# Output projection, second norm and down product with channels on the partitions, in a hybrid attention and SwiGLU block

## The chip, the core and the metric

One core of a Trainium2 chip runs the whole block in one launch. Its engines work side by side: TensorE (PE: matmuls, and PEld for its weight loads), VectorE (DVE), ScalarE (ACT), GpSimd (POOL) and SyncE (SP, which here only issues DMAs). The metric is the device time of one execution in microseconds, the median of several runs. The time before is 1010.89 us (three runs, 1010.83 to 1011.81).

## The reference, cut to what matters

```python
def rms_norm(x, g):
    y = xf * lax.rsqrt(jnp.mean(xf * xf, axis=-1, keepdims=True) + EPS)
    return y * g

def reference(x, ...):            # x: 1 x 1024 tokens x 1024 channels, float32
    h = rms_norm(x, norm1_g)
    q, k, v, u = split(h @ w_in)  # 512 wide each
    a = neighbourhood_attention(rms_norm(q), rms_norm(k), v, rpb)
    p = multiscale_pool(u, w_pool, pool_scale)
    x = x + concat([a, p]) @ w_out
    h2 = rms_norm(x, norm2_g)
    x = x + (silu(h2 @ w_gate) * (h2 @ w_up)) @ w_down   # 1024 -> 2816 -> 1024
    return x
```

The sum of squares of the second norm runs over the channels of one token.

## The kernel before

All products run in a reduced float32 format with each operand split into a high and a low half (`split`: ScalarE casts the high half, VectorE subtracts to get the low one); one product is three matmuls, high by high, high by low, low by high (`mm3`, `product`, `down`). The gate, up and down products are done as 2x2 block products with seven instead of eight multiplications: operands "11", "12", "21", "22" are blocks, and "s1" to "s4" (of the weights) and "t1" to "t4" (of the activations) are sums and differences of blocks. `sum_w` and the "s4" line of `cook_w` form the weight sums on POOL; `cook_w` splits them. The activations' blocks: the first half of the tokens (512) and the second half, by the first 512 channels and the last.

Around the change the program runs in these stages:

- Attention, interleaved with the projection (`g_dense`). `w_out(t, nh, cs, n)` adds up the output projection of token tile t (128 tokens) and channel half nh in a PSUM bank `pw`, and one VectorE add (L814) adds it to the residual in `x2[t]`, a tile of 128 tokens by 1024 channels that a DMA has filled with x.
- The second norm (`norm2(tt)`, two token tiles at a time). ScalarE issues the DMA that parks `x2[t]` in `x2d`, squares it with a running sum per token (L954), and Ln and Exp of two numbers per partition give the reciprocal root (L96, L97). VectorE scales the tile by the token's factor and by the channels' weights `g2b` (L962).
- Turns. The gate and up products need channels on the partitions, so `turn_op` turns each 128x128 block on TensorE into a PSUM bank `ht` (`tr`, L90), and `split` reads it from there into the operand `ACTO[o]`, called b11, bt2 and so on (`b`, `bt` in the profile). Each of seven operands takes 16 turns: 112. For the second half of the tokens the differences are formed before the turn: a0, t2 on VectorE (L975, L976), two more on POOL (L977, L978).
- The gate and up products. Index i runs over 22 blocks (gate and up in turn). For the first four (EARLY) the program does `first` and `second` (PSUM bank `x`, operands "11" and "21", which need the first half's norm alone) for all four, and then the rest of each (`rest`: banks `y`, `z`, `w`, operands t2, t3, t1, t4, 22, all of which need the second half). ScalarE takes Silu of the gate (L1056), VectorE or POOL multiplies (L1060). Results are parked in DRAM (`park`, `gsd`).
- The down product (`down`, `PLAN`): again seven products in three groups; its results are added to `x2` loaded back from `x2d`, and `ship` sends them out.

The order on each engine is set when the program is built, by a scheduler that plays the program through, except where the program pins it (attention, down product). PSUM has eight banks: pools `mmp` (3), `stp` (4), `pop` (1). SBUF tiles come from 45 slots that are used in turn, so a DMA into a slot waits for the last reader of what was there.

Of the kernel before, what the change touches and what calls it, by code (L numbers as in the profile page):

```python
# [9 lines left out]
F32 = mybir.dt.float32  # L10
# [39 lines left out]
def hybrid_block(ctx, tc, xT, xt, w1, wu, rpbx, wpool, wout, wgu, wd, g2, sm, out):  # L50
# [21 lines left out]
    sm_sb = cp.tile([P, 14], F32, name="sm_sb")  # L72
    g1_sb, psc_sb, gqk = sm_sb[:, 0:8], sm_sb[:, 8:12], sm_sb[:, 12:14]
# [724 lines left out]
    def w_out(t, nh, cs, n):  # L798
        ps = bank(stp if n else mmp, f"pw_{t}_{nh}_{n}")
        ns = slice(nh * 512, nh * 512 + 512)  # L800
        ts_ = slice(t % 4 * P, t % 4 * P + P)
        hf = t // 4
# [11 lines left out]
        nc.vector.tensor_tensor(out=x2[t][:, ns], in0=ps, in1=x2[t][:, ns], op=ALU.add)  # L814
# [5 lines left out]
    def g_dense():  # L820
# [5 lines left out]
        x2.extend(slot(F32, f"x2_{t}") for t in range(4))  # L826
        for t in range(4):
            nc.sync.dma_start(out=x2[t], in_=xt[t])
# [18 lines left out]
        for t in range(4):  # L847
# [4 lines left out]
            x2.append(slot(F32, f"x2_{4 + t}"))  # L852
            nc.sync.dma_start(out=x2[4 + t], in_=xt[4 + t])
# [52 lines left out]
    for t in range(4):  # L906
        for nh in range(2):
            for _ in w_out(t, nh, (2, 3), 1):
                pass
# [5 lines left out]
    sm2 = ctx.enter_context(tc.tile_pool(name="sm2", bufs=3))  # L915
    rg = ctx.enter_context(tc.tile_pool(name="rg", bufs=RING))
    x2d = [dp.tile([P, DM], F32, name=f"x2d_{t}") for t in range(NT)]
    gsd = [dp.tile([7, P, 512], F32, name=f"gsd_{f}") for f in range(NPF)]
    g2b = slot(F32, "g2b")
    nc.sync.dma_start(out=g2b, in_=g2.to_broadcast([P, DM]))  # L920
    junk = slot(F32, "junk")
    banks2 = (mmp, mmp, pop)
    nbk = 0
    ACTO = {}
    h2 = {}
# [6 lines left out]
    def turn_op(o, tt, srcs):  # L932
        nonlocal nbk
        ts_ = slice(tt % 2 * 256, tt % 2 * 256 + 256)
        for q in range(2):
            pt = bank(banks2[nbk % 3], f"ht_{o}_{tt}_{q}")
            nbk += 1
            for s in range(2):
                for i in range(2):
                    k = 2 * q + s  # L940
                    tr(
                        pt[:, s * 256 + i * P : s * 256 + i * P + P], srcs[i][:, k * P : k * P + P], ident
                    )
            hi, lo = ACTO[o][q]
            split(hi[:, :, ts_], lo[:, :, ts_], pt.rearrange("p (s n) -> p s n", s=2))

    def norm2(tt):
        v = sm2.tile([P, 16], F32, name=f"v2_{tt}", tag="v2")[:, :2]
        y = sm2.tile([P, 16], F32, name=f"y2_{tt}", tag="y2")[:, :2]
        for i in range(2):  # L950
            t = 2 * tt + i
            ss = sm2.tile([P, 16], F32, name=f"s2_{t}", tag="s2")[:, :1]
            nc.scalar.dma_start(out=x2d[t], in_=x2[t])
            nc.scalar.activation(junk, x2[t], AF.Square, accum_out=ss)  # L954
            nc.vector.tensor_scalar(
                out=v[:, i : i + 1], in0=ss, scalar1=1.0 / DM, scalar2=EPS, op0=ALU.mult, op1=ALU.add
            )
        rsqrt(sm2, y, v, 2, f"h{tt}")
        for i in range(2):
            t = 2 * tt + i  # L960
            h2[t] = x2[t]
            nc.vector.scalar_tensor_tensor(  # L962
                out=h2[t], in0=x2[t], scalar=y[:, i : i + 1], in1=g2b, op0=ALU.mult, op1=ALU.mult
            )
        if tt < 2:
            for o, j in (("11", 0), ("21", 1)):
                turn_op(o, tt, [h2[2 * tt + i][:, 512 * j : 512 * j + 512] for i in range(2)])
            return
        t2 = slot(F32, f"t2_{tt}", [P, 2, 512])
        lows, highs = [], []  # L970
        for i in range(2):
            t = 2 * tt + i
            a, b_ = h2.pop(t - 4), h2.pop(t)
            a0, a1, b0, b1 = a[:, :512], a[:, 512:], b_[:, :512], b_[:, 512:]
            nc.vector.tensor_tensor(out=a0, in0=b0, in1=a0, op=ALU.subtract)  # L975
            nc.vector.tensor_tensor(out=t2[:, i], in0=b1, in1=a0, op=ALU.subtract)  # L976
            nc.gpsimd.tensor_tensor(out=b0, in0=b1, in1=b0, op=ALU.subtract)  # L977
            nc.gpsimd.tensor_tensor(out=a1, in0=a1, in1=t2[:, i], op=ALU.subtract)  # L978
            lows.append((a0, a1))
            highs.append((b0, b1))  # L980
        src = {
            "t2": [t2[:, 0], t2[:, 1]],
            "t3": [h[0] for h in highs],
            "t1": [h[0] for h in lows],
            "22": [h[1] for h in highs],
            "t4": [h[1] for h in lows],
        }
        for o in src:
            turn_op(o, tt - 2, src[o])
# [81 lines left out]
    def rest(i, y, z, w, after, mid=None):  # L1071
        a, b_ = res[i]
        u2, u3 = a[:, 1], b_[:, 1]
# [3 lines left out]
        add(u2, ps, u2)  # L1077
        pz = bank(z, f"z_{i}")
# [38 lines left out]
    norm2(0)  # L1117
    norm2(1)
    for i in range(2):
        fetch_w(i)  # L1120
        cook_w(i, "11")
        cook_w(i, "12")
        sum_w(i)
    for nh in range(2):
        for t in range(6 - 2 * nh, 8):
            for _ in w_out(t, nh, eight, 2):
                pass
    for o in ("t2", "t3", "t1", "22", "t4"):
        act_op(o)
    norm2(2)  # L1130
    norm2(3)
    xs = [bank(stp, f"x_{i}") for i in range(EARLY)]
    for i in range(EARLY):
        if i == 2:
            for j in range(2, EARLY):
                fetch_w(j)
                cook_w(j, "11")
                cook_w(j, "12")
                sum_w(j)
# [4 lines left out]
    ring = (stp, stp, mmp, stp, stp)  # L1144
    nrk = 0
    LATE = ("s2", "s3", "s1", "22", "s4")
    for o in LATE:
        cook_w(0, o)
    for i in range(EARLY):
# [3 lines left out]
        three = []  # L1153
        for _ in range(3):
            three.append(ring[nrk % 5])
            nrk += 1
        nxt = i + 1

        def after(o):
            cook_w(nxt, o)  # L1160
            if nxt == EARLY and o == "s2":
                cook_w(nxt, "11")
            if nxt == EARLY and o == "s1":
                cook_w(nxt, "12")

        rest(i, *three, after)
# [3 lines left out]
    for i in range(EARLY, len(MF)):  # L1170
# [12 lines left out]
        rest(i, *yzw, after, mid=lambda: second(i, ps))  # L1183
# [6 lines left out]
    def quad(c, i, l):  # L1190
        return x2[c + 4 * i][:, 512 * l : 512 * l + 512]
# [101 lines left out]
    def ship(c, i, l, n0=0, n1=512):  # L1293
        t = c + 4 * i
        ns = slice(512 * l + n0, 512 * l + n1)
        nc.sync.dma_start(out=out[t][:, ns], in_=x2[t][:, ns])
# [11 lines left out]
    for t in range(NT):  # L1308
        x2[t] = slot(F32, f"x2r_{t}")
# [105 lines left out]
```

## Time and profile before

| | |
|---|---|
| median of 3 runs | 1010.89 us |
| profiled execution: time, span | 1011.3 us, 1009.5 us |
| PE busy | 997.8 us (99%), 4905 matmuls |
| DVE, ACT, POOL busy | 660.4, 415.8, 387.9 us |
| granted TensorE clock | 1.00 |

The span is the time from the first to the last instruction; about 2 us of the execution's time lie around it. Rows of a timeline give start, duration, engine, line, operation, what is written and read (out<-in), the shape, and in square brackets how long the engine stood idle before it and what ended that. The groups by line give count, busy time, mean ns, and idle time before. A matmul's duration includes its way through the array, so the distance of two starts is what it costs.

### The profile page before, as it was taken

The page shows a single profiled execution, that of the slowest core. Times are in us where ns is not written, and L with a number is a line of the kernel's source. Part 1 is how long each engine was busy: PE and PEld are TensorE (multiplying, and loading weights), DVE is VectorE, ACT ScalarE, POOL GpSimd, SP SyncE. Part 2 cuts the span into 40 slices and gives each one's busy share as a digit, 9 for nine tenths or more (in the row PEclk, how much of TensorE's full clock was granted, in tenths as well). Part 3 has the DMA queues.
Part 4 walks back from the last instruction along what each step waited for, and adds up shares of the span by engine and source line. Part 5 has one row for each costly group of instructions (what it writes and reads, how often), then busy time and mean ns, then how long its engine had stood idle before and what let it go on. Part 6 is the DMA issues. An engine that isn't in the chain of part 4 may idle for free.

```text
span 1009.5 us, 13495 instructions
## 1 busy us (share of the span) xinstructions
PE 997.8 (99%) x4905; PEld 851.1 (84%) x4905; DVE 660.4 (65%) x1087; ACT 415.8 (41%) x817; POOL 387.9 (38%) x427
## 2 busy tenths in 40 slices
PE   9999999999999998999999999999999999999998
PEld 9988989998888887888888888888888888888887
DVE  5677777657853769668555555555462599888872
ACT  6633666656642346333233233233242255442500
POOL 0001534332520436367846846846733400000170
PEclk9999999999999999999999999999999999999999
DMA  9412742346811321223313312322317984373302
GB/s 348 189 58 86 222 119 82 90 145 245 266 64 72 117 104 53 94 105 108 143 62 111 134 70 107 133 73 105 130 49 242 360 283 125 108 247 105 125 32 94
DMA packets 55298, 136.41 MB, mean 135 GB/s; under 512 B 5888, under 2 KB 14848, under 8 KB 55232
## 3 DMA queue, kind: packets, MB, share of 16 engines
q1 hardware_dynamic: 47152, 106.97, 31.7%
q0 software_dynamic: 6784, 24.38, 6.5%
q10 hardware_dynamic: 1296, 4.20, 1.0%
q8 instruction: 38, 0.62, 0.2%
q14 instruction: 28, 0.23, 0.1%
HBM read 98.57 MB, written 32.77 MB: 130 GB/s over the span
## 4 chain that ended last, share of the span: by engine, by line
PE 92%; DVE 3%; ACT 2%; DMA 1%; issue 1%; SPq 0%; DVEq 0%
PE x L85 12%; PE z L85 12%; PE w L85 12%; PE pj L85 10%; PE pw L85 8%; PE pc L85 6%; PE pa L85 6%; PE y L85 6%; PE pd L85 6%; PE pu L85 4%; PE pb L85 3%; PE po L85 3%; PE s L85 2%; PE pt L90 1%; DMA raw_w<-in_w 1%
## 5 line engine op out<-in xcount | busy, mean ns | idle before, releaser
L85 PE MATMUL x<-b_h,w 128*128 128x512 f32 x352 | 115.7, 391 | 0.0
L85 PE MATMUL pw<-wo,mx 128*128 128x512 f32 x384 | 91.6, 393 | 0.5 <-DVE kl L112 0.4
L85 PE MATMUL pj<-w1h,xh 128*128 128x384 f32 x256 | 87.1, 344 | 2.1 <-DVE vnl L298 1.7
L85 PE MATMUL pj<-w1l,xh 128*128 128x384 f32 x256 | 84.8, 335 | 1.0 <-DVE w1l L112 1.0
L618 POOL TENSOR_SCALAR e<-e,r 64x128 f32<-64x128 f32 (+2 forms) x96 | 52.8, 566 | 83.7 <-DVE r L613 45.9
L85 PEld LDWEIGHTS pw<-wo,mx 128*128 128x128 f32 x384 | 70.8, 188 | 15.4 <-DVE kl L112 0.8
L85 PE MATMUL pj<-w1h,xl 128*128 128x384 f32 x256 | 83.8, 336 | 0.0
L1341 POOL TENSOR_TENSOR x2r<-x2r,u 128x512 f32<-128x512 f32 x12 | 23.8, 2021 | 149.7 <-DVE u L1299 149.7
L85 PEld LDWEIGHTS x<-b_h,w 128*128 128x128 f32 x352 | 66.0, 188 | 13.5
L1060 POOL TENSOR_TENSOR ur<-ur,gr 128x512 f32<-128x512 f32 x33 | 53.5, 1624 | 39.8 <-issue 22.0
L85 PE MATMUL x<-b_l,w 128*128 128x512 f32 x176 | 68.6, 390 | 0.0
L112 DVE TENSOR_TENSOR w_s<-sa,w_s 128x512 fp32r<-128x512 f32 x44 | 48.3, 1098 | 26.3 <-ACT w_s L111 26.2
L111 ACT CAST a_h<-raw_a 128x1024 fp32r<-128x1024 f32 (+1 forms) x42 | 41.0, 979 | 49.4 <-PE pc L85 13.8
L85 PE MATMUL z<-bt_h,w 128*128 128x512 f32 x176 | 57.7, 389 | 0.0
L85 PE MATMUL z<-bt_h,w_s 128*128 128x512 f32 x176 | 57.7, 389 | 0.0
L85 PE MATMUL y<-bt_h,w_s 128*128 128x512 f32 x176 | 57.7, 389 | 0.0
L85 PE MATMUL w<-bt_h,w_s 128*128 128x512 f32 x176 | 57.7, 389 | 0.0
L85 PE MATMUL w<-b_h,w_s 128*128 128x512 f32 x176 | 57.7, 389 | 0.0
L1010 POOL TENSOR_TENSOR sa<-raw_g,raw_g 128x512 f32<-128x512 f32 x11 | 14.7, 1333 | 105.1 <-DMA raw_g<-in_wgu 59.2
L112 DVE TENSOR_TENSOR a_l<-raw_a,a_h 128x1024 fp32r<-128x1024 f32 (+1 forms) x42 | 49.9, 1191 | 3.4 <-ACT a_h L111 3.1
L85 PEld LDWEIGHTS pj<-w1h,xh 128*128 128x128 f32 x256 | 48.2, 189 | 3.9 <-DVE vnl L298 2.6
L85 PEld LDWEIGHTS pj<-w1l,xh 128*128 128x128 f32 x256 | 48.1, 188 | 1.4 <-DVE w1l L112 1.4
(258 smaller groups left out, 2684.1 us busy)
## 6 DMA issues: line engine op xcount, KB each, us to landing
raw_a<-gsd SPq DMA_DIRECT2D x77, 256.0 KB, 3.5
raw_g<-in_wgu SPq DMA_DIRECT2D x22, 512.0 KB, 3.9
raw_u<-in_wgu SPq DMA_DIRECT2D x22, 512.0 KB, 3.9
gsd<-gr POOLq DMA_DIRECT2D x22, 512.0 KB, 4.0
raw_d<-in_wd SPq DMA_DIRECT2D x20, 512.0 KB, 4.1
nb<-in_rpbx SPq DMA_DIRECT2D x24, 384.0 KB, 3.8
raw_w<-in_w SPq DMA_DIRECT2D x15, 384.0 KB, 4.6
gsd<-ur POOLq DMA_DIRECT2D x11, 512.0 KB, 3.2
```

Source lines behind the costliest of these rows:

```text
L85: i = nc.tensor.matmul(*a, **k)
L90: i = nc.tensor.transpose(*a)
L111: keep(nc.scalar.copy(h, src))
L112: keepd(nc.vector.tensor_tensor(out=l, in0=src, in1=h.bitcast(F32), op=ALU.subtract))
L618: nc.gpsimd.tensor_scalar(out=out, in0=in0, scalar1=s1, scalar2=1.0, op0=ALU.mult, op1=ALU.mult)
L1010: tt(out=s1, in0=r0[:, 1], in1=r1[:, 1], op=ALU.add)
L1060: eng.tensor_tensor(out=res[i][c][:, l], in0=src, in1=g, op=ALU.mult)
L1341: nc.gpsimd.tensor_tensor(out=q, in0=q, in1=U2[c], op=ALU.add)
```

## The change

Channels stay on the partitions from the output projection to the output, and no turn is left after attention.

- `w_out` has the weights as the standing operand and the mixed activations as the moving one. Its bank holds 128 channels by 512 tokens. `x2[n]` is a tile of 128 partitions by two channel tiles by 512 tokens, filled from `xT`; tiles 0 to 3 are the first half of the tokens, 4 to 7 the second.
- A token's sum of squares now runs across partitions and tiles. `square` takes squares on ScalarE (128x1024), POOL adds them up, `tok_sum` splits the sum and multiplies it by a matrix of ones on TensorE, so that every partition holds the token's sum (`ss`). For the second half the last tile goes to the product in two pieces of its own.
- `scale2` forms the factor as 128x512 values: a VectorE read of the sum, Ln and Exp on ScalarE, three VectorE steps. `norm2` scales with it and with the channel's weight (a column of `sm_sb`): eight operations of 128x512 a half.
- The operands are split directly from SBUF, 128x1024 at a time; the differences are formed 128x1024 at a time (L985, L986 on VectorE, L988, L989 on POOL).
- The four early blocks do all their `y` products first (`part_y`), and then `z` and `w` (`part_zw`).
- `down` exchanges its two operands, and the output's layout follows.

```diff
+        o, hf = 4 * nh + t % 4, t // 4
         for i, c in enumerate(cs):
             mm3(
                 ps,
-                mix[c, hf, 0][:, ts_],
-                mix[c, hf, 1][:, ts_],
-                wo[c, nh, 0],
-                wo[c, nh, 1],
+                wo[c, nh, 0][:, os_],
+                wo[c, nh, 1][:, os_],
+                mix[c, hf, 0],
+                mix[c, hf, 1],
...
-    def turn_op(o, tt, srcs):
...
+    def tok_sum(hf, src, first, last):
+        if first:
+            ps2[hf] = bank(pop, f"ss_{hf}")
+        hl = slot(F32R, f"sq_hl_{hf}_{first}_{last}", [P, 2, 512])
+        split(hl[:, 0], hl[:, 1], src)
+        for n in range(2):
+            mm(ps2[hf], ones, hl[:, n], start=first and n == 0, stop=last and n == 1)
+
+    def square(hf, q):
+        x = x2[q + 4 * hf]
+        nc.scalar.dma_start(out=x2d[q + 4 * hf], in_=x)
+        s = sq[hf, q] = slot(F32, f"sq_{hf}_{q}", [P, 2, 512])
+        if q == 3 and hf:
+            for i in range(2):
+                nc.scalar.activation(s[:, i], x[:, i], AF.Square)
+                tok_sum(hf, s[:, i], False, i == 1)
+            return
+        nc.scalar.activation(s, x, AF.Square)
+        acc = sq[hf, 0]
+        add_ = nc.gpsimd.tensor_tensor
+        if q:
+            add_(out=acc, in0=acc, in1=s, op=ALU.add)
+        if q == 3 - hf:
+            add_(out=acc[:, 0], in0=acc[:, 0], in1=acc[:, 1], op=ALU.add)
+            tok_sum(hf, acc[:, 0], True, hf == 0)
+
+    def scale2(hf):
+        n = slot(F32, f"n2_{hf}", [P, 2, 512])
+        n2[hf] = y = slot(F32, f"y2_{hf}", [P, 512])
+        v, a = n[:, 0], n[:, 1]
+        nc.vector.tensor_scalar(out=v, in0=ps2[hf], scalar1=1.0 / DM, scalar2=EPS, op0=ALU.mult, op1=ALU.add)
+        nc.scalar.activation(a, v, AF.Ln)
+        nc.scalar.activation(y, a, AF.Exp, scale=-0.5)
+        nc.vector.tensor_tensor(out=a, in0=y, in1=y, op=ALU.mult)
...
+    def norm2(hf, q):
+        x = x2[q + 4 * hf]
+        for i in range(2):
+            k = 2 * q + i
+            nc.vector.scalar_tensor_tensor(
+                out=x[:, i], in0=x[:, i], scalar=g2_sb[:, k : k + 1], in1=n2[hf], op0=ALU.mult, op1=ALU.mult
+            )
...
+    def sums_t(q):
+        a0, a1, b0, b1 = x2[q], x2[2 + q], x2[4 + q], x2[6 + q]
+        t2 = slot(F32, f"t2_{q}", [P, 2, 512])
+        nc.vector.tensor_tensor(out=a0, in0=b0, in1=a0, op=ALU.subtract)
+        nc.vector.tensor_tensor(out=t2, in0=b1, in1=a0, op=ALU.subtract)
+        split_op("t2", q, t2)
+        nc.gpsimd.tensor_tensor(out=b0, in0=b1, in1=b0, op=ALU.subtract)
+        nc.gpsimd.tensor_tensor(out=a1, in0=a1, in1=t2, op=ALU.subtract)
...
     for i in range(EARLY):
-        if i == 2:
-            for j in range(2, EARLY):
-                fetch_w(j)
...
         first(i, xs[i])
         if i % 2:
             for j in (i - 1, i):
                 second(j, xs[j])
+    act_op("t2")
+    for q in range(2):
+        norm2(1, q)
+        norm2(1, q + 2)
+        sums_t(q)
+    cook_w(0, "s2")
+    cook_w(1, "s2")
+    sum_w(3)
...
+    for i in range(EARLY):
+        part_y(i, stp, lambda o: None)
...
-                    a[:, y % 2, sl],
-                    b_[:, y % 2, n0:n1],
+                    b_[:, y % 2, sl],
+                    a[:, y % 2, n0:n1],
```

Where the instructions stand now is read from the built programs. Names in the rows: x_0 to x_7 are the `x2` tiles, x_44.. and x_42.. the PSUM banks of `first` and `second`, bt_0 and bt_1 the two channel halves of an operand t, w_11 and w_s the split weights, sa the weight sums.

TensorE, among the x products of the early blocks. Before, turns of the second half stand between them:

```order
L90 MATMUL ht_t_1_0_4428<-ident,x_2_3117 128x128
L90 MATMUL ht_t_1_0_4428<-ident,x_3_3118 128x128
L85 MATMUL x_4472<-b_0_h,w_11_4534 128x512
L85 MATMUL x_4472<-b_0_l,w_11_4534 128x512
L90 MATMUL ht_1_0_4442<-ident,x_6_3719 128x128
L90 MATMUL ht_1_0_4442<-ident,x_7_3768 128x128
```

And now, behind 36 x products, five of the six products with ones, and the sixth after nine more:

```order
L85 MATMUL ss_4166<-sq_hl_True_False,ones_3966 128x512 x2
L85 MATMUL ss_4166<-sq_hl_False_False,ones_3966 128x512 x2
L85 MATMUL ss_4166<-sq_hl_False_True,ones_3966 128x512
L85 MATMUL x_4271<-b_0_h,w_12_4027 128x512
L85 MATMUL x_4271<-b_0_l,w_12_4027 128x512
L85 MATMUL x_4271<-b_0_h,w_12_4027 128x512 x2
```

The last ones product thus stands 50 products behind the first x product, and 51 (three of x_1 and 48 of x_2 and x_3) follow it before the first y.

ScalarE, at the norm of the second half's last tiles. Before:

```order
L954 ACTIVATE junk,s_7_4379<-x_7_3768 128x1024
L96 ACTIVATE rsq_h_4383<-v_3_4373 128x2
L1065 COPY gr_0_4474<-x_4470 128x512
L97 ACTIVATE y_3_4374<-rsq_h_4383 128x2
L111 CAST bt_0_h<-ht_t_0_0_4303 128x2x256
```

And now:

```order
L1056 ACT_TABLE_LOAD
L1056 ACTIVATE gr_0_4274<-x_4270 128x512
L111 CAST w_12_4245<-raw_g_1_4240 128x512
L111 CAST w_11_4252<-raw_u_0_4248 128x512
L111 CAST w_12_4255<-raw_u_1_4250 128x512
L964 ACT_TABLE_LOAD
L964 ACTIVATE n_1_4258<-n_1_4258 128x512
L1065 COPY gr_0_4330<-x_4272 128x512
L965 ACT_TABLE_LOAD
L965 ACTIVATE y_1_4259<-n_1_4258 128x512
L1065 COPY ur_0_4345<-x_4273 128x512
L1056 ACT_TABLE_LOAD
```

The first Silu now comes ahead of this Ln and Exp, and three more table loads stand in the queue, one of them between Ln and Exp.

VectorE, from the read of the sum to the first y operand (now):

```order
L963 TENSOR_SCALAR n_1_4258<-ss_4166 128x512
L112 TENSOR_TENSOR w_12_4255<-raw_u_1_4250,w_12_4255 128x512
L966 TENSOR_TENSOR n_1_4258<-y_1_4259 128x512
L967 SCALAR_TENSOR_TENSOR n_1_4258<-n_1_4258 128x512
L968 SCALAR_TENSOR_TENSOR y_1_4259<-n_1_4258,y_1_4259 128x512
L974 SCALAR_TENSOR_TENSOR x_4_3587<-x_4_3587,sm_sb,y_1_4259 128x512 x2
...
L985 TENSOR_TENSOR x_0_3115<-x_4_3587,x_0_3115 128x1024
L985 TENSOR_TENSOR x_1_3117<-x_5_3628,x_1_3117 128x1024
L1060 TENSOR_TENSOR ur_0_4345<-x_4273,gr_0_4330 128x512
L986 TENSOR_TENSOR t_0_4394<-x_6_3719,x_0_3115 128x1024
L112 TENSOR_TENSOR bt_0_l<-t_0_4394,bt_0_h 128x1024
L986 TENSOR_TENSOR t_1_4405<-x_7_3768,x_1_3117 128x1024
```

Before, this work stood in two parts, tiles 4 and 5 ahead of the last add of the projection:

```order
L962 SCALAR_TENSOR_TENSOR x_4_3587<-x_4_3587,y_2_4277,g2b 128x1024
L962 SCALAR_TENSOR_TENSOR x_5_3628<-x_5_3628,y_2_4277,g2b 128x1024
L975 TENSOR_TENSOR x_0_3115<-x_4_3587,x_0_3115 128x512
L814 TENSOR_TENSOR x_6_3719<-pw_1_2_4204,x_6_3719 128x512
L975 TENSOR_TENSOR x_1_3116<-x_5_3628,x_1_3116 128x512
```

All of it now stands behind the sum. On POOL the four subtractions L988 and L989 of 128x1024 follow sum_w(2), with sum_w(3) behind them.

More of the change, by code (lines that the diff above doesn't have):

```diff
@@ L914, in hybrid_block @@
     tq_.close()
-    sm2 = ctx.enter_context(tc.tile_pool(name="sm2", bufs=3))
     rg = ctx.enter_context(tc.tile_pool(name="rg", bufs=RING))
-    x2d = [dp.tile([P, DM], F32, name=f"x2d_{t}") for t in range(NT)]
+    x2d = [dp.tile([P, 2, 512], F32, name=f"x2d_{t}") for t in range(NT)]
     gsd = [dp.tile([7, P, 512], F32, name=f"gsd_{f}") for f in range(NPF)]
[L919 to L923, printed above, removed]
+    ones = slot(F32R, "ones2", [P, P])
+    nc.gpsimd.memset(ones.bitcast(F32), 1.0)
     ACTO = {}
-    h2 = {}
     def act_op(o):
@@ L1182, in hybrid_block @@
         after("11")
-        rest(i, *yzw, after, mid=lambda: second(i, ps))
+        part_y(i, yzw[0], after)
+        part_zw(i, *yzw[1:], after, mid=lambda: second(i, ps))
         if i % 2:
```

161 lines of the change are left out of this document (62 added, 99 removed).

## The prediction

> **What bounds the kernel now.** I read the page first (busy shares, granted clock, chain), then TensorE's waits, then the stretch from 335 to 426 us, where the second norm and its turns stand.
>
> ```profile
> PE   997.8 (99%) x4905; PEld 851.1 (84%) x4905; DVE 660.4 (65%) x1087; ACT 415.8 (41%) x817; POOL 387.9 (38%) x427
> ...
> PEclk9999999999999999999999999999999999999999
> ...
> PE 92%; DVE 3%; ACT 2%; DMA 1%; issue 1%; SPq 0%; DVEq 0%
> ...
> PE ht_t L90 <- DVE bt_l L112: 1.5, 1, 1.5
> ...
> PE ht_t L90 <- DVE b_l L112: 1.0, 1, 1.0
> ...
> L85 PE MATMUL x<-b_h,w 128*128 128x512 f32 x352 | 115.7, 391 | 0.0
> L85 PE MATMUL pw<-wo,mx 128*128 128x512 f32 x384 | 91.6, 393 | 0.5 <-DVE kl L112 0.4
> ```
>
> TensorE is the bound: it is busy all the time at the full granted clock, and the chain that ends last is TensorE work. So an instruction taken from it is worth its own time, as long as it still finds operands. The last two rows show both operand orders already in use (weights moving in pw, activations moving in x) at 391 to 393 ns, so exchanging the two in the output projection and in the down product costs nothing on TensorE, whose cover it does not need.
>
> The next rows are the stage. The first pair counts the products (L85), the second the turns (L90), in two stretches: from the first turn to the end of the output projection, and from the first gate product x to the first product y.
>
> ```profile
> 335.39:364.36 28.97, 26.21 (x113) 1.00 0.29 109
> 364.36:395.81 31.45, 20.68 (x85) 1.00 0.27 92
> ...
> 335.39:364.36 28.97, 3.98 (x32) 1.00 0.29 109
> 364.36:395.81 31.45, 10.65 (x80) 1.00 0.27 92
> ...
> 380.41 0.66 PE L90 MATMUL ht_t<-ident,x 128*128 128x128 f32 x4 [0.96 <-DVE b_l L112]
> 382.56 0.63 PE L90 MATMUL ht_t<-ident,x 128*128 128x128 f32 x4 [1.49 <-DVE bt_l L112]
> ...
> 395.82 0.39 PE L85 MATMUL y<-bt_h,w_s 128*128 128x512 f32 x1
> ...
> 404.14 2.72 PE w L85 x12
> ```
>
> **What goes.** Twelve products of 128x512 take 2.72 us, 0.227 each. The two stretches last 60.42 us and hold 112 + 84 products of their own (each count includes one that was still running at its start): 196 x 0.227 = 44.4. The other 16.0 us go to the change: 2.45 of waiting (0.96 + 1.49) and 13.5 for 112 turns, 0.12 each with what they cost at the seams.
>
> **What comes on TensorE.** Eight products with ones, 8 x 0.227 = 1.8 us. If nothing waited, the kernel would gain 16.0 - 1.8 = 14.2 us.
>
> **What comes in the chain.** Before, each pair of token tiles is normalised as soon as it is projected: tiles 4 and 5 at 357 us (the first row of the next fence), before the projection's end at 364. With channels on the partitions a token's sum needs all eight channel tiles, so the norm of the second half begins after the last projection product, and the products y wait for all of it. The cover is 96 x products and 6 products with ones: 102 x 0.227 = 23.1 us from the first x product, which I call T = 0 (361.2 us in the old count: 364.36, less the 3.6 us that 32 turns took of the first stretch, 28.97 - 112 x 0.227, and plus two ones products, 0.45).
>
> The durations come from these rows: the adds of x, norm, subtraction and split on VectorE (starts 1.13 apart for 128x1024, 0.60 for 128x512), and ScalarE's table load, activation and the two cast sizes.
>
> ```profile
> 357.22 2.48 DVE L962 SCALAR_TENSOR_TENSOR x<-x,y,g2b 128x1024 f32<-128x1024 f32 x2
> ...
> 382.33 1.28 DVE L976 TENSOR_TENSOR t<-x,x 128x512 f32<-128x512 f32 x2
> ...
> 924.31 1.22 DVE L112 TENSOR_TENSOR a_l<-raw_a,a_h 128x1024 fp32r<-128x1024 f32 x1
> 925.44 1.22 DVE L112 TENSOR_TENSOR dbt_l<-dt,dbt_h 128x1024 fp32r<-128x1024 f32 x1
> ...
> 375.35 1.28 ACT L1056 ACT_TABLE_LOAD   x1
> 376.64 0.60 ACT L1056 ACTIVATE gr<-x 128x512 f32<-128x512 f32 x1
> ...
> L111 ACT CAST a_h<-raw_a 128x1024 fp32r<-128x1024 f32 x35 | 36.8, 1051 | 49.4 <-PE pc L85 13.8 <-PE pd L85 9.5 <-PE pa L85 7.9
> L111 ACT CAST w_s<-sa 128x512 fp32r<-128x512 f32 x44 | 27.3, 620 | 37.1 <-PE x L85 14.7 <-DVE w_s L112 11.5 <-PE z L85 8.7
> ```
>
> In the new order of the queues:
> - The last ones product stands behind 50 products (36 x, five ones, nine x): done at T = 11.8. Its squares (two activations, three casts, an add before and a subtraction behind) are ready by about 7, so its place decides.
> - VectorE's read of the sum stands behind the gate multiply of x_1 (three products later, 12.3 + 0.7) and one weight split: done at 14.4.
> - ScalarE: Ln to 15.0, the copy of x_2 queued behind it to 15.5, a table load of 1.28, Exp to 17.5. Before, Ln and Exp ran ahead of the first Silu and no load stood between them; now one does.
> - VectorE: three Newton steps (1.8) and eight scalings (4.9) to 24.2; two subtractions, one gate multiply and the first t2, to 28.3.
> - ScalarE casts it (29.4), VectorE splits it and forms the second t2 (31.7), ScalarE casts that (32.7) and then the first weight sum: T = 33.3.
>
> TensorE is out of x products at 23.1 and gets y at 33.3: a wait of 10.2 us with nobody in VectorE's way. With it the gain falls to about 14.2 - 10.2 = 4.0, and 3.2 after the 0.8 us of short waits while the first y products get their low halves.
>
> [...]
>
> **The first half's norm** I cost at nothing: its last ones product stands 91 projection products (20.6 us) ahead of the first x product, and the work between them (one read of the sum, Ln, Exp, three Newton steps, eight scalings, four weight splits and two adds of 0.6 each, four splits of 1.14) comes to 16.6. If that cover were gone by turns with POOL, the first x would wait by what is over 20.6. SP loses one load (g2b) and issues the same eight x loads. The raw weights for i = 2, 3 wait for projection weights' buffers, free by T = 0, and ScalarE casts them from T = 6:
>
> ```profile
> raw_g<-in_wgu SPq DMA_DIRECT2D x22, 512.0 KB, 3.9
> ```
>
> So they land in time, with 2 us to spare.
>
> **The price that decides: VectorE and POOL together.** Before, 28 splits read the turned tile from PSUM. Now 14 splits of double size read two SBUF operands, and so do the eight scalings. What that means beside POOL is in these rows (VectorE first, then POOL).
>
> ```profile
> 362.15 2.37 DVE L976 TENSOR_TENSOR t<-x,x 128x512 f32<-128x512 f32 x2
> ...
> 396.31 1.78 DVE L112 TENSOR_TENSOR w_s<-sa,w_s 128x512 fp32r<-128x512 f32 x1
> 398.01 1.78 DVE L112 TENSOR_TENSOR w<-raw_g,w 128x512 fp32r<-128x512 f32 x1
> ...
> 957.60 0.68 DVE L1299 TENSOR_TENSOR u<-pb,u 128x512 f32<-128x512 f32 x1
> 958.20 1.72 DVE L112 TENSOR_TENSOR dbt_l<-raw_d,dbt_h 128x1024 fp32r<-128x1024 f32 x1
> ...
> 338.24 1.31 POOL L1010 TENSOR_TENSOR sa<-raw_g,raw_g 128x512 f32<-128x512 f32 x1 [39.47 <-PE pw L85]
> ...
> 362.30 1.67 POOL L977 TENSOR_TENSOR x<-x 128x512 f32<-128x512 f32 x1 [0.63 <-DVE x L975]
> ...
> 395.81 1.74 POOL L1012 TENSOR_TENSOR raw_u<-raw_u 128x512 f32<-128x512 f32 x1
> 397.51 1.74 POOL L1023 TENSOR_TENSOR raw_u<-raw_u,sa 128x512 f32<-128x512 f32 x1
> ...
> 954.40 23.81 POOL L1341 TENSOR_TENSOR x2r<-x2r,u 128x512 f32<-128x512 f32 x12 [149.75 <-DVE u L1299]
> ```
>
> A VectorE operation on two SBUF operands takes 0.69 alone and 1.78 beside POOL, 1.1 more, nearly a whole POOL operation (1.25 apart); a pair of t takes 2.37 and not 1.28. An operation with a PSUM operand stays at 0.68 (957.60) while POOL runs. So the two take turns, operation by operation.
>
> Behind the norm POOL holds four 128x512 operations of sum_w(2), then four subtractions of 128x1024 (about 2.5 each, twice the row; an estimate) and four of sum_w(3). In the chain up to the scalings' end I take 3.3 us for the turns with sum_w(2) (three of four met, 1.1 each). From there, T = 24.2 + 3.3 = 27.5, until the weight split that the second z product needs, VectorE has 14 operations of 1.14 and nine of 0.60 on two SBUF operands, 21.4, and POOL 4 x 2.5 + 4 x 1.25 = 15.0. Taking turns, they end at 27.5 + 36.4 = 63.9. TensorE's order then has 46 products (10.4) left of the 218 up to the end of the first s4 product: 74.3. Before, the same 218 took 31.45 for 84 and 134 x 0.227 = 30.4 for the others, 61.8, from a start 3.1 later. So 74.3 - 61.8 - 3.1 = **9.4 us more**. Bounds: side by side without turns, 3.2 us less; turns with gaps (the big POOL operation first each time, VectorE idle behind ScalarE's casts: four casts of 1.05, and one turn of 1.25 lost), 5.3 more, so 14.7. I take 9.4, since the rows show turns and no case of two running at full speed. Against the profiled execution (span 1009.5, time 1011.3) that gives 1020.7; it lies 0.4 above the median of 1010.89, so I say 1020.
>
> **The rivals.**
> 1. No turns on the large operations: POOL gives way inside 128x1024. Only the 10.2 us wait remains, and the time is 1011.3 - 3.2, about 1008. For it: no row shows a POOL operation of this size. Against: all rows of the smaller size. It decides if y starts before about T = 36.5 and z follows without a wait; partial turns give 1010 to 1014. Chance 0.24.
> 2. TensorE slows down after the long wait. At its start it was slow:
>
> ```profile
> 1.19 4.00 PE L85 MATMUL warm_ps<-warm 128*128 128x256 f32 x17 [1.19 <-DVE warm L470]
> ...
> 304.10 0.28 PE L85 MATMUL po<-pt_l,vsh 128*128 128x256 f32 x1
> 304.21 0.28 PE L85 MATMUL po<-pt_h,vsl 128*128 128x256 f32 x1
> ```
>
> 17 products of 256 columns took 3.8 us to the next one, 0.22 each, where later ones follow at 0.11 to 0.12. If a wait of 10 to 16 us brings that back, the next 3.8 us do half the work: 1.9 us more, and as much again after a second gap: 1022 to 1024. Against: the one pair of waits inside the kernel, 2.45 us, left the clock at 1.00. Chance 0.28. [...]
> 3. The chain hides after all (the sum is done early, y finds its operands): 1011.3 - 14.2 = 997. Against: TensorE's own order puts the sum at T = 11.8, and the chain behind it holds 21 us. Chance 0.06.
>
> **The numbers.** Forecast without slowing 0.42, with it 0.28, rival 1 0.24, rival 3 0.06. A measurement of this kernel tells 0.2% (2 us) from no change. Rival 1's lower part (1008) gives 0.15 to faster, its partial turns 0.06 to same and 0.03 to slower. Faster 0.15 + 0.06 = 0.21, same 0.06, and 0.04 from the forecast's low edge, slower the other 0.69. Range 1007 to 1027: rival 1 below, gaps in the turns (1026) and slowing above.
>
> **What would show it.** Right: no ht rows; TensorE idle for 10 to 18 us before the first y, released by ScalarE's w_s or bt_h; table loads before L964 and L965; scalings and splits at 1.1 us and more above their lone time while L988 and L989 run. Wrong: y directly behind x; splits at 1.22 throughout; or the x products themselves waiting for the first half's norm, which would cost more than all this.

## The result, and the profile after

The changed kernel takes 1020.13 us (median of four runs, 1019.67 to 1023.12), the kernel before 1010.86 (four runs, 1010.75 to 1011.81): ratio 1.0096, 95% interval 1.0076 to 1.0116. It is slower by 9.3 us; the forecast was 1020. The profiled execution took 1023.12 us, span 1021.3; it reached the stage of the change 3.6 us later than another execution of the same program (first x product at 363.75 us against 360.14), so places in the stage are counted from its first x product, T = 0.

The page of the changed kernel: busy times, granted clock, shares of the chain, one group.

```profile
PE 992.1 (97%) x4801; PEld 844.1 (83%) x4801; DVE 675.2 (66%) x1069; ACT 421.3 (41%) x799; POOL 407.7 (40%) x431
...
PEclk9999999999999996899999999999999999999999
...
PE 86%; DVE 9%; ACT 2%; DMA 1%; issue 1%; SPq 0%; ACTq 0%; DVEq 0%
...
L85 PE MATMUL pw<-mx,wo 128*128 128x512 f32 x384 | 91.1, 392 | 0.6 <-DVE kl L112 0.4
```

TensorE has 104 matmuls fewer (112 turns gone, 8 ones products added) and is busy 5.7 us less; yet the span is longer, the chain has 9% of VectorE instead of 3%, and the clock has a dent. The operand exchange cost nothing (pw 392 ns, 393 before; x starts without a wait, and no DMA stands among the waits). TensorE's waits in the stage (engine, line, what it waited for: total, times, longest):

```profile
PE y L85 <- ACT w_s L111: 17.4, 1, 17.4
...
PE y L85 <- DVE w_s L112: 1.5, 1, 1.5
...
PE z L85 <- DVE w_s L112: 0.2, 1, 0.2
```

By stretches (length; busy PE, PEld, DVE, ACT, POOL with counts; clock; DMA share; GB/s):

```profile
361.00:385.00 24.00, 23.94 (x105) 19.44 (x104) 17.43 (x16) 14.16 (x21) 13.70 (x8) 1.00 0.34 119
385.00:405.00 20.00, 2.65 (x12) 1.91 (x11) 17.74 (x16) 3.23 (x5) 11.59 (x5) 0.63 0.03 13
405.00:415.00 10.00, 8.46 (x21) 6.15 (x22) 10.00 (x7) 6.82 (x10) 8.31 (x5) 0.55 0.01 2
```

From 385 to 405 us TensorE stands while VectorE and POOL work; from 405 to 415 it works at about half the clock. The same on TensorE's timeline: first x, last ones product, first y, the slow pace, the last wait.

```profile
363.75 0.39 PE L85 MATMUL x<-b_h,w 128*128 128x512 f32 x1
...
375.48 0.39 PE L85 MATMUL ss<-sq_hl_False_True,ones 128*128 128x512 f32 x1
...
404.78 0.79 PE L85 MATMUL y<-bt_h,w_s 128*128 128x512 f32 x1 [17.35 <-ACT w_s L111]
...
408.40 1.22 PE L85 MATMUL y<-bt_h,w_s 128*128 128x512 f32 x2 [1.54 <-DVE w_s L112]
409.41 0.63 PE L85 MATMUL y<-bt_l,w_s 128*128 128x512 f32 x1
409.84 1.05 PE L85 MATMUL y<-bt_h,w_s 128*128 128x512 f32 x2
...
427.95 0.73 PE L85 MATMUL z<-bt_h,w_s 128*128 128x512 f32 x2 [0.24 <-DVE w_s L112]
```

409.41 to 409.84 is 0.43 us for one product, where one costs 0.227 otherwise. VectorE in the same stretch, and then three of POOL's four subtractions, with one lone POOL operation of that size from the first half's norm:

```profile
393.21 0.68 DVE L1060 TENSOR_TENSOR ur<-x,gr 128x512 f32<-128x512 f32 x1
393.81 2.76 DVE L986 TENSOR_TENSOR t<-x,x 128x1024 f32<-128x1024 f32 x1
397.68 2.17 DVE L112 TENSOR_TENSOR bt_l<-t,bt_h 128x1024 fp32r<-128x1024 f32 x1 [1.11 <-ACT bt_h L111]
399.78 3.35 DVE L986 TENSOR_TENSOR t<-x,x 128x1024 f32<-128x1024 f32 x1
404.24 2.42 DVE L112 TENSOR_TENSOR bt_l<-t,bt_h 128x1024 fp32r<-128x1024 f32 x1 [1.11 <-ACT bt_h L111]
406.58 3.44 DVE L112 TENSOR_TENSOR w_s<-sa,w_s 128x512 fp32r<-128x512 f32 x2
409.94 4.53 DVE L112 TENSOR_TENSOR bt_l<-x,bt_h 128x1024 fp32r<-128x1024 f32 x2
...
416.80 1.21 DVE L112 TENSOR_TENSOR bt_l<-x,bt_h 128x1024 fp32r<-128x1024 f32 x1
```

```profile
327.18 2.40 POOL L954 TENSOR_TENSOR sq<-sq,sq 128x1024 f32<-128x1024 f32 x1 [25.75 <-ACT sq L950]
...
392.23 6.54 POOL L988 TENSOR_TENSOR x<-x,x 128x1024 f32<-128x1024 f32 x2 [7.91 <-DVE x L985]
399.30 2.75 POOL L989 TENSOR_TENSOR x<-x,t 128x1024 f32<-128x1024 f32 x1
```

A VectorE operation of 128x1024 on two SBUF operands takes 2.2 to 3.4 us beside POOL and 1.21 once POOL is done (416.80). The one that reads PSUM (ur, 393.21) takes its lone 0.68 in the middle of a POOL subtraction.

### The profile page after: what moved, and what is told of

Its sections match the earlier page's. It is cut to its first block, busy times and chain, and to the rows that moved or that the text cites. A ratio compares the mean times of both kernels' runs of the same rounds, so it can differ in the third digit from the quotient of the medians.

```text
span 1021.3 us, 13246 instructions
## 1 busy us (share of the span) xinstructions
PE 992.1 (97%) x4801; PEld 844.1 (83%) x4801; DVE 675.2 (66%) x1069; ACT 421.3 (41%) x799; POOL 407.7 (40%) x431
## 4 chain that ended last, share of the span: by engine, by line
PE 86%; DVE 9%; ACT 2%; DMA 1%; issue 1%; SPq 0%; ACTq 0%; DVEq 0%
PE z L85 11%; PE w L85 11%; PE pj L85 10%; PE x L85 10%; PE pw L85 7%; PE pc L85 6%; PE pa L85 6%; PE pd L85 6%; PE y L85 5%; PE pu L85 3%; PE pb L85 3%; PE po L85 3%; PE s L85 2%; PE pt L90 1%; DVE b_l L112 1%; DVE bt_l L112 1%
## 5 line engine op out<-in xcount | busy, mean ns | idle before, releaser
L85 PE MATMUL pw<-mx,wo 128*128 128x512 f32 x384 | 91.1, 392 | 0.6 <-DVE kl L112 0.4
L85 PEld LDWEIGHTS pw<-mx,wo 128*128 128x128 f32 x384 | 71.0, 188 | 15.6 <-DVE kl L112 0.9
L85 PE MATMUL y<-bt_h,w_s 128*128 128x512 f32 x176 | 60.1, 406 | 18.9 <-ACT w_s L111 17.4
L1060 POOL TENSOR_TENSOR ur<-ur,gr 128x512 f32<-128x512 f32 x33 | 52.6, 1594 | 36.4 <-issue 22.0
L112 DVE TENSOR_TENSOR w_s<-sa,w_s 128x512 fp32r<-128x512 f32 x44 | 45.1, 1028 | 26.0 <-ACT w_s L111 25.9
L111 ACT CAST a_h<-raw_a 128x1024 fp32r<-128x1024 f32 (+1 forms) x42 | 41.0, 978 | 49.5 <-PE pc L85 13.8
L85 PE MATMUL z<-bt_h,w_s 128*128 128x512 f32 x176 | 57.7, 390 | 0.2 <-DVE w_s L112 0.2
L85 PEld LDWEIGHTS y<-bt_h,w_s 128*128 128x128 f32 x176 | 34.5, 197 | 27.4 <-ACT w_s L111 17.8
```

Source lines behind the costliest of these rows:

```text
L85: i = nc.tensor.matmul(*a, **k)
L111: keep(nc.scalar.copy(h, src))
L112: keepd(nc.vector.tensor_tensor(out=l, in0=src, in1=h.bitcast(F32), op=ALU.subtract))
L1060: eng.tensor_tensor(out=res[i][c][:, l], in0=src, in1=g, op=ALU.mult)
```

## The experiments

Ratios are to the kernel before, run on the same chip, with the 95% interval. The changed kernel itself, run again beside some of them, took 1020.23 us: ratio 1.0080 (1.0068 to 1.0092).

> The changed kernel once more, unaltered, as the measure for the runs beside it and for an execution of the usual length: 0.9 to 1.0% over the kernel before, first wait before y 17 to 18 us, products y 0.43 apart behind it.

**Is POOL the reason?** The changed kernel without POOL's four subtractions and the weight sums for i = 2, 3:

```diff
-        nc.gpsimd.tensor_tensor(out=b0, in0=b1, in1=b0, op=ALU.subtract)
-        nc.gpsimd.tensor_tensor(out=a1, in0=a1, in1=t2, op=ALU.subtract)
+        if i in (2, 3):
+            sums[i]["s1"], sums[i]["s2"] = r1[:, 1], r0[:, 0]
+            return
```

> Leaves out of the changed kernel what POOL computes during the wait: the four subtractions of 128x1024 (L988, L989) and the weight sums for i = 2 and 3 (six of the eight 128x512 operations; raw weights are used instead). VectorE, ScalarE and TensorE do the same work in the same order. If VectorE and POOL take turns, VectorE's subtractions and splits fall to 1.2 us each, the wait of TensorE from 17.35 to about 10, and the time by 7 to 9 us, to 1011 to 1013 (half clock after the wait stays). If the wait is the chain's own length, at most 1 us goes: 1019 to 1020. If POOL's operations cost VectorE only a little, between.

1010.62 us, 0.9988 (0.9979 to 0.9997): all of the loss is gone. Its waits in the stage, and VectorE in its chain:

```profile
PE y L85 <- ACT w_s L111: 11.1, 1, 11.1
```

```profile
388.82 1.22 DVE L986 TENSOR_TENSOR t<-x,x 128x1024 f32<-128x1024 f32 x1
391.15 1.23 DVE L112 TENSOR_TENSOR bt_l<-t,bt_h 128x1024 fp32r<-128x1024 f32 x1 [1.11 <-ACT bt_h L111]
```

So 9.5 us are the price of POOL's work as it stood here. 6.2 of them lie in this one wait (17.4 less 11.1), where VectorE's operations on SBUF operands fall back to their lone times; the rest lies in the slow pace and the waits behind it. The run also takes away two short stops of ScalarE for POOL's weight sums (1.3 and 1.1 us), so not quite all of it is turns. The wait of 11.1 us that is left is the chain's own.

**The four subtractions alone,** all work kept, moved to VectorE behind the first two weight-sum splits:

```diff
-        nc.gpsimd.tensor_tensor(out=b0, in0=b1, in1=b0, op=ALU.subtract)
-        nc.gpsimd.tensor_tensor(out=a1, in0=a1, in1=t2, op=ALU.subtract)
+        return a1, b0, b1, t2
...
+    with tc.issue_after(low[-1].ins):
+        for a1, b0, b1, t2 in abt:
+            nc.vector.tensor_tensor(out=b0, in0=b1, in1=b0, op=ALU.subtract)
+        for a1, b0, b1, t2 in abt:
+            nc.vector.tensor_tensor(out=a1, in0=a1, in1=t2, op=ALU.subtract)
```

> The changed kernel with one thing moved: the four 128x1024 subtractions that make the operands of y's products (two on each half of the activations) run on VectorE behind its splits of the first two weight sums, instead of on GpSimd. Everything is still computed. Theory (GpSimd is what makes the chain before y long): VectorE's two t and two bt_l of the chain fall back from 2.17 to 3.35 us each to about 1.2; the wait of the y products falls from 17.4 to about 12 us; VectorE has 4 x 1.14 = 4.6 us more work of its own behind the first y product, of which some waits return; 1011 to 1014 us. Rival (VectorE's own load is the bound, and moving work onto it costs what the turns cost): first wait shorter, but the waits before the later y and z products longer by as much; 1019 to 1022 us.

1014.95 us, 1.0038 (1.0024 to 1.0051): some 5 us won (5.3 by the medians, 4.2 by the two ratios), though VectorE has 4.6 us more work of its own. The first y waits 13.8 us, and the waits behind it are of 0.6 us at most:

```profile
PE y L85 <- ACT w_s L113: 13.8, 1, 13.8
```

The wait is 1.8 longer than expected because sum_w(3) now moves up beside the chain (second t 2.28 us, second bt_l 2.33), and the time is 1 us above the range.

**Is it the slow clock?** Seventy filler products into a bank that nobody reads, between x and y:

```diff
+    keepw = bank(mmp, "keepw")
+    for _ in range(70):
+        tc.keep_in_program_order(nc.tensor.matmul(keepw, ones, ACTO["11"][0][0][:, 0], start=True, stop=True))
```

> Adds to the changed kernel 70 products of 128x512 with the ones tile, into a PSUM bank that nobody reads, between the last product x and the first product y: 70 x 0.227 = 15.9 us of work inside the wait of 17.35 us. Nothing that the kernel computes is left out. If the long wait slows TensorE's clock, the products y run 0.23 apart from the first one on instead of 0.43 for some 22 of them, and the time falls by 3 to 4.5 us, to 1015.6 to 1017.1. If the 0.43 is only the pace at which operands arrive (VectorE busy 8.5 of those 10 us), the pace stays and the time is 1020 within 1 us.

1021.0 us, 1.0091 (1.0077 to 1.0105): nothing won. But the fillers ended 1.67 us early, a second wait of 2.58 followed, and behind it the products stood 0.43 apart again, until 410.6:

```profile
402.10 0.50 PE L85 MATMUL y<-bt_h,w_s 128*128 128x512 f32 x1 [1.67 <-ACT w_s L111]
...
405.71 1.22 PE L85 MATMUL y<-bt_h,w_s 128*128 128x512 f32 x2 [2.58 <-DVE w_s L112]
```

So it didn't settle the question. With 76 fillers and 14 more behind the second y product:

> As the run with 70 filling products, but with no gap left: 76 of them (17.3 us) before the first product y, and 14 more (3.2 us) between its second and third product, where TensorE waits for the low half of the weight sum. If the slow pace of 0.43 behind the waits is the clock's answer to an idle TensorE, all products y run 0.23 apart, 14 products gain 0.2 each, and the time falls by up to 2.8 us against the changed kernel (less by what z then waits for its operands: 1 to 2.8). If it is the pace of operands or of the product itself, the pace stays 0.43 and the time stays within 0.5 us.

1025.86 us, 1.0136 (1.0122 to 1.0149): outside both ranges, a miss. But now the y products stand 0.23 apart, so the slow pace is the clock after waiting:

```profile
401.96 3.35 PE L1159 MATMUL keepw<-b_h,ones 128*128 128x512 f32 x14
405.15 0.63 PE L85 MATMUL y<-bt_h,w_s 128*128 128x512 f32 x2
405.61 0.40 PE L85 MATMUL y<-bt_l,w_s 128*128 128x512 f32 x1
...
411.82 0.74 PE L85 MATMUL y<-bt_h,w_s 128*128 128x512 f32 x2 [1.04 <-DVE w_s L112]
```

What was won came back as a wait for VectorE (411.82): the first z starts at T = 56.8, in the run with 70 fillers at 57.7. The time as a whole is no measure here, since the build also put a VectorE add behind other splits. For it z waited 3.2 us, and behind that wait 16 products stood 0.43 us apart again.

**The table load.** Silu of the first quarter of blocks 0 and 2 replaced by a copy, so that no load stands between Ln and Exp:

```diff
-            nc.scalar.activation(res[i][c][:, l], src, AF.Silu)
+            nc.scalar.activation(res[i][c][:, l], src, AF.Copy if i < 4 and c == l == 0 else AF.Silu)
```

> Replaces, in the changed kernel, the Silu of the first quarter for i = 0 and 2 by a copy, so that ScalarE loads no table between the norm's steps; that part of the result is not the reference's. The load before Ln (376.44) ended 0.8 us before its operand came, the one before Exp (379.91) stood in the chain: 1.28 us. If the chain sets the wait, first y and time move by 1.3 us, to 1018.8. If the wait is set by something beside the chain (POOL, ScalarE's queue), nothing moves: 1020. Only if both loads cost, 2.6.

1020.55 us, 1.0086 (1.0072 to 1.0099): no gain; y starts at T = 40.7 instead of 41.0. The Newton steps came earlier and so met more of POOL's sum_w(2): the three took 1.46, 1.66 and 1.67 us, where the changed kernel has 1.29, 1.67 and 0.69.

**The turns alone.** The kernel before without its 112 turns, the splits reading the unturned tiles in SBUF:

```diff
-            pt = bank(banks2[nbk % 3], f"ht_{o}_{tt}_{q}")
...
-            split(hi[:, :, ts_], lo[:, :, ts_], pt.rearrange("p (s n) -> p s n", s=2))
+            split(hi[:, :, ts_], lo[:, :, ts_], srcs[q].rearrange("p (s n) -> p s n", s=2))
```

> The kernel before with its 112 turns left out and nothing else moved: the 28 splits read the normalised tiles from SBUF as they lie, not the turned ones from PSUM, so the products get unturned operands. It shows what the removal gives in the order of before, where each pair of token tiles is normalised as soon as it is there. Without turn taking of VectorE and POOL: 16.0 us less, 995. With turn taking: from 364 to 426 us VectorE (46.6 busy) and POOL (28.7) hold 75 us of work together, some 6 of it on PSUM operands, in 62 us less 13.5: most of the gain is lost in waits before y and z, and the time is 1000 to 1015.

1018.14 us, 1.0058 (1.0045 to 1.0070): 13.5 us of work taken from the engine that bounds the kernel, nothing added, and it is 6 us slower, 3 us above the range. Its waits, and VectorE:

```profile
PE x L85 <- DVE w L112: 6.9, 1, 6.9
PE x L85 <- ACT w L111: 5.5, 1, 5.5
```

```profile
378.73 1.75 DVE L112 TENSOR_TENSOR bt_l<-x,bt_h 128x512 fp32r<-128x512 f32 x1
```

Read from PSUM, these splits had been out of POOL's way (0.68 beside it, at 388.26 in the kernel before); read from SBUF they take 1.75 beside it (0.69 alone). With POOL's two subtractions and weight sums 2 and 3 gone as well:

> The kernel before without its 112 turns (splits read the unturned tiles from SBUF), and also without what POOL computes in that stretch (the subtractions L968 and L969 and the weight sums for i = 2 and 3, raw weights instead). Without turns alone it was 6 us slower than before, with waits of 17 us before x and y. If turn taking of VectorE and POOL made those waits, they fall to a few us and the time to 996 to 1002, near 1011 - 16. If they come from the order of the queues (weights for i = 2 and 3 behind the splits) or from late weights, most of them stay: 1010 to 1017.

1007.36 us, 0.9951 (0.9937 to 0.9965), between the two ranges: 10.8 us of the loss was POOL. Of the 13.5 us 4.7 are won; the rest stands in waits of x, most of them for weights that ScalarE and VectorE split behind the operands (4.9 and 3.0).

**A better order.** The changed kernel's arithmetic, reordered: the reciprocal root and its square kept in PSUM, the splits for the first weight sums ahead of the norm, the first half of t2 finished before the second begins, early Silu behind the norm, POOL's subtractions after its weight sums.

> The changed kernel with the same arithmetic and another order and place of the norm's steps: the last adds of x ahead of the splits of operand 21; the sum read at once; Ln, Exp and the square of y (on ScalarE now) ahead of the weight casts and of Silu, so that no table load stands between; the rsqrt's result in PSUM, so that the Newton steps and the scalings have a PSUM operand; the weight sums for y cast and split during the x products; scaling, subtraction and split of the first half of t2 before the second half's scaling; POOL's weight sums first, then L988 twice, then L989 twice. By the theory (chain length and turn taking, both shortened) the last sum is done at T = 5, t2 at about T = 15 and 22, before TensorE is out of x products at 23.3: no long wait, no slow clock, and of the 14.2 us of removed TensorE work most is gained: 997 to 1003, with short waits for z as the unknown. If the wait has another cause (late weights, the sheer sum of VectorE's and POOL's work), it is found again before y or z and the time is 1008 to 1018.

1010.55 us, 0.9988 (0.9979 to 0.9996): in the second range, with a wait found again, 4.2 us for a cast of ScalarE ahead of the first y. Still, order alone won nearly 10 us against the changed kernel. Next, the last squares' sum earlier, POOL's weight sums held back until the first Newton step and its subtractions until t2 is formed:

> The reordered kernel again, with what its trace showed late put right, arithmetic unchanged: the splits of operand 21 into VectorE's gaps ahead of the last add of x; the squares of the last channel tile ahead of the cast of the running sum; the ones products three to six products further back, so that TensorE doesn't wait for them; the weight casts and splits for y and for i = 2 into the gaps while the sum, Ln, Exp and the square are under way; POOL's weight sums held until the first Newton step and its subtractions until t2 is formed, so that they don't take turns with the chain. The run before it waited 4.4 us before y, 2.5 us for ones products and operand 21, and ran some 20 products at the slow pace; its 218 products ended at T = 65.4, those of the changed kernel at 74.7. If chain and turns are the whole cause, they now end at T = 52 to 56 and the time is 998 to 1003, some 1% under the kernel before. If the sum of VectorE's and POOL's work in the stage is itself too long, the waits come back before z and w and the time stays above 1006.

1013.46 us, 1.0021 (1.0012 to 1.0030), a miss. The first y does start at T = 24.3 (41.0 in the changed kernel), so the chain can be hidden. But the held-back work meets the next operands, and the waits stand before z:

```profile
PE z L85 <- DVE w_s L115: 3.5, 1, 3.5
...
PE z L85 <- DVE ur L1077: 2.0, 1, 2.0
```

```profile
392.89 5.68 DVE L115 TENSOR_TENSOR w_s<-sa,w_s 128x512 fp32r<-128x512 f32 x2
```

Two splits that take 1.29 alone took 5.68 beside POOL's subtractions. So an order can hide the chain, but in the two tried VectorE's and POOL's work came due a little later; that no order can hide that work was not shown. Last, the same with the subtractions on VectorE, where they also stand at other places in its queue, behind splits of t2:

```diff
-        tc.keep_in_program_order(nc.gpsimd.tensor_tensor(out=b0, in0=b1, in1=b0, op=ALU.subtract))
...
-        g = nc.gpsimd.tensor_tensor(out=a1, in0=a1, in1=t2, op=ALU.subtract)
...
+            nc.vector.tensor_tensor(out=b0, in0=b1, in1=b0, op=ALU.subtract)
...
+                    nc.vector.tensor_tensor(out=a1, in0=a1, in1=t2, op=ALU.subtract)
```

> The reordered kernel of the run before (e9_reordered, 1013.5 us) with the four 128x1024 subtractions on VectorE (1.14 us each by the row of the lone one) instead of GpSimd (2.4 us alone, 2.8 us and more beside VectorE). Everything is still computed. Theory (the shared work of VectorE and GpSimd is the bound, and a subtraction holds it twice as long on GpSimd): some 16 us of turn taking fall to 8 or so, the waits of 3.5 and 2.0 before z go, the 218 products end near 56 instead of 64.9 us; 999 to 1004 us. Rival (VectorE alone is full by then): waits before z stay at 5 us or grow, 1010 to 1015 us.

1007.21 us, 0.9963 (0.9950 to 0.9975): faster than both kernels, 3 us short of the range. The 218 products end at 62.2, not 56. Its waits, then the stretch from the first y on (busy PE, DVE and so on as above) and a row behind the last wait:

```profile
PE w L85 <- DVE w_s L115: 3.0, 1, 3.0
PE y L85 <- DVE bt_l L115: 1.7, 1, 1.7
PE y L85 <- ACT bt_h L113: 1.0, 1, 1.0
```

```profile
386.00:402.00 16.00, 14.25 (x53) 10.91 (x54) 15.97 (x20) 7.64 (x11) 2.46 (x4) 0.89 0.10 34
402.00:424.00 22.00, 19.05 (x72) 15.17 (x71) 20.43 (x26) 13.47 (x21) 2.89 (x3) 0.84 0.14 48
```

VectorE is busy for 15.97 of 16 us with POOL nearly idle: now it is full by itself. And behind the waits the products stand 0.43 apart for a while, which costs some 5 us in all. The last run put fillers into those waits (3, 7 and 22):

> The kernel of the run before last but for one thing (e10_sub_vector, 1007.2 us, ratio 0.9963): 32 filler products of 128x512 into a bank that nobody reads, 3 ahead of the first y product (which waited 0.95 us), 7 behind it (1.7 us), 22 ahead of the third product of the first w (3.0 us). In e10 the y products behind the second wait stood 0.43 us apart until 392.1 us and those of w and z behind the third until 412.7 us, some 12 of each, 5.2 us more than at 0.227. Theory A (the slow pace is the clock after waiting, and VectorE, busy for 16.0 of 16.0 us from 386 on, holds what comes before w): all products 0.227 us apart; the 2.6 us won in y come back as a longer wait before w, the 2.6 us behind it stay; end of the 218 products near 59.7 instead of 62.2 us, 1004 to 1005.5 us. Theory B (the clock alone decides): both are won, 57 us, 1001 to 1003. Theory C (the pace has no part in the end, something else is as late): 62 us or more, 1006.5 to 1008.

1007.37 us, 0.9953 (0.9939 to 0.9967): the same as without them, as the third theory has it, with the 218 products ending at T = 61.1 instead of 62.2. All products now follow at 0.23, clock 1.00. The first w needs a split that VectorE ends at 407.79, T = 45.6, in the run before at T = 45.6 too: the time won in y did turn into a longer wait, which is the part of the first theory that holds. But the 22 fillers ran 1.9 us past that point, so the 2.6 us behind it were mostly given away by my own count:

```profile
404.73 5.15 PE L1063 MATMUL keepw<-b_h,ones 128*128 128x512 f32 x22
409.71 0.61 PE L85 MATMUL w<-bt_h,w_s 128*128 128x512 f32 x2
```

```profile
407.10 0.69 DVE L116 TENSOR_TENSOR w_s<-sa,w_s 128x512 fp32r<-128x512 f32 x1
```

What the clock is worth there, at most 2 to 3 us, stays open.

## Why the prediction came out right, step by step

**The sum.** Forecast: 218 products done at T = 74.3, 9.4 us more than before. Measured: 74.8 and, in the second execution, 74.7; there the last of the 218 products ends at 434.9 us against 426.2 before (the 61.8 us behind 364.36), 8.7 more. The time differs by 9.3. The stages ahead and behind are as before within 1 us, as costed.

**What goes and comes on TensorE.** 16.0 less 1.8, 14.2 us, held within 1 us. The run without POOL's work shows it: 1010.62, less its wait of 11.1 and 2.8 us of slow pace (17 products in 6.7 us), is 996.7. The forecast without any wait was 997; against the kernel before beside that run (1011.85) it is 15.2 us less.

**The chain.** The last ones product starts at T = 11.7 and ends at 12.1 (forecast: done at 11.8). Its squares were ready at 9.0, not at 7, but its place in the queue decided, as forecast. ScalarE:

```profile
376.44 1.28 ACT L964 ACT_TABLE_LOAD   x1
378.51 0.63 ACT L964 ACTIVATE n<-n 128x512 f32<-128x512 f32 x1 [0.80 <-DVE n L963]
...
379.91 1.28 ACT L965 ACT_TABLE_LOAD   x1
381.21 0.63 ACT L965 ACTIVATE y<-n 128x512 f32<-128x512 f32 x1
```

Ln starts at 14.8 (14.4), its own load hidden while ScalarE waited; Exp ends at 18.1 (17.5). The scalings end at 27.3 (27.5). With nobody in VectorE's way the wait was to be 10.2; it measured 11.1. Behind the load Exp starts at once, 1.30 us after the load's start, so the row's 1.28 was the right price. Its worth was not: counted as 1.28 in the chain, it was worth 0.3 at the first y and nothing in the time, since behind it VectorE met POOL.

**The price that decided: right total, wrong terms.** From the scalings' end to the split that the second z product needs, the forecast had 36.4 us: 21.4 of VectorE's own work and 15.0 of POOL's, added up. Measured are 36.9 (391.02 to 427.95), and z did wait for that split, 0.24 us, at T = 64.2 (63.9). But of these 36.9 VectorE's own work was 24.5, standing idle behind ScalarE's two casts 2.2, and turns 10.2, the sum of what the six rows from 393.81 to 409.94 have over their lone times (1.54, 0.95, 2.13, 1.20, 2.15, 2.18). Of POOL's work 4.8 less was met than forecast. VectorE's was under-counted by 3.1: five operations with a PSUM operand in this stretch (0.6 us each, as at 393.21) are not among the 21.4. The idle time stands only in the upper bound (whose four casts and one turn, 4 x 1.05 and 1.25, make 5.45, not 5.3). Before the scalings' end, 3.3 us of turns were forecast and 1.6 met. So the mechanism was right, but that the total came out to the microsecond is luck: the errors of its terms cancelled.

**The rivals.** No turns on the large operations (1008): false, by the rows of 2.17 to 3.35 and by the run without POOL's work, which shows about what it would have given, 1010.6. I had no row of that size and gave it 0.24. The rows show which operands are held up: with two in SBUF 3.35 us against 1.22 without POOL's work, with one in PSUM 0.68 beside POOL (393.21) as without it (415.60).

Slow clock after the wait (1022 to 1024): true in the rows, false in the time. Behind the waits some 17 products took 3.7 us more than at 0.227. Two dips were foreseen; it was one stretch of half clock, from 390.2 to 414.1 us, with slow products behind the first wait and behind the second. But the operands of z came hardly sooner with fillers, so it cost about 1 us by the two filler runs (first z at 57.7 and 56.8). The clock's loss counted only where nothing else was late.

Chain hidden (997): not in this order. Reordered, it is hidden but for 2.6 us (0.95 and 1.69 ahead of y, in the fast reordered kernel), and still not 997, since VectorE's and POOL's work comes due a little later.

**Costed at nothing:** operand exchange, first half's norm, raw weights: each as forecast in the time. In the first half's norm VectorE and POOL did take turns (three splits in 8.99 us from 358.19 on, 3 x 1.14 alone), but x still started without a wait.

## What to carry to other kernels

Work taken off the engine that bounds a kernel may have been shielding another: a turn through PSUM cost TensorE 0.12 us a block and kept VectorE's splits out of POOL's way (0.68 us each; read from SBUF, 1.75). Before a change moves operands from PSUM to SBUF, add up VectorE's two-operand SBUF work and POOL's over the stretch in which the results are due, and set that sum against the gain. Reordering hid a part of it here (1020 to 1010.6 us), and the rest came back as waits elsewhere. What shrank it was giving POOL's large operations (2.40 us) back to VectorE (1.14): 5 us in the changed kernel, 6 us in the reordered one.

## What was not expected of the hardware

TensorE's clock fell after short waits. In the kernel before, waits of 0.96 and 1.49 us with four turns between left it at 1.00. In the fast reordered kernel waits of 0.95 and 1.69 us, with two products between, brought products 0.43 apart for some 3.5 us, and the clock over the 16 us from 386 on was 0.89:

```profile
386.06 1.00 PE L85 MATMUL y<-bt_h,w_s 128*128 128x512 f32 x2 [0.95 <-ACT bt_h L113]
388.75 0.50 PE L85 MATMUL y<-bt_l,w_s 128*128 128x512 f32 x1 [1.69 <-DVE bt_l L115]
...
389.93 0.63 PE L85 MATMUL y<-bt_h,w_s 128*128 128x512 f32 x1
390.35 0.63 PE L85 MATMUL y<-bt_l,w_s 128*128 128x512 f32 x1
390.78 1.05 PE L85 MATMUL y<-bt_h,w_s 128*128 128x512 f32 x2
```

In the first reordered kernel 0.95 and 1.26 us, with three products between, did the same:

```profile
371.27 0.51 PE L85 MATMUL x<-b_l,w 128*128 128x512 f32 x1 [1.26 <-DVE b_l L114]
...
372.51 0.63 PE L85 MATMUL x<-b_h,w 128*128 128x512 f32 x1
372.93 0.63 PE L85 MATMUL x<-b_l,w 128*128 128x512 f32 x1
```

Around the wait of 17.35 us in the changed kernel the clock was 1.00 until 390.2 us, 2.8 us after TensorE had run out of work, and 0.50 from there to 414.1, 9.3 us past the first y. So waits that add up to 2.45 us left the clock alone in one run, and behind waits of 2.21 and 2.64 us in two others products stood 0.43 apart. What tells them apart was not shown.
